# A decoder layer's dense expert stage: one block's sum held in PSUM, value weights in 4 KB packets, gates loaded eight chunks at a time

## The chip, the core and the metric

The kernel runs on one core of one Trainium2 chip. The metric is the time of one execution on the device, in microseconds (us). Engines are named as in the profile: PE is the matrix engine (PEld its weight loads), DVE the vector engine, ACT the scalar engine, POOL the GpSimd engine, SP the sync engine, which here only issues DMAs. The core's DMAs run on 16 DMA engines.

## What is computed

The reference is one post-norm decoder layer over 1024 tokens of width 1024, in float32: a mixer (attention heads beside recurrent heads), then a mixture over 16384 single-neuron experts. The change touches only the latter:

```python
q = (xt @ w_q)...                       # 8 heads, two halves of 128
s = einsum('thpd,hpnd->thpn', q, sub_keys)
...                                     # two top-16 lists, their 256 sums, top 16 of these: idx, gates
def blk(args):                          # a block of 128 tokens, 128 experts per token
    u = u_tab[idx_b]
    h = gelu(einsum('td,ted->te', x_b, u)) * g_b
    return einsum('te,ted->td', h, v_tab[idx_b])
...
x = layer_norm(ALPHA * x + y)
```

## The kernel before

The 1024 tokens are eight blocks of 128. Blocks 0, 1, 6 and 7 (`GATHER`) are done as the reference says: for each of a token's 128 experts POOL issues an indirect DMA that brings one row of 4 KB per partition (a "gather", 512 KB, into a tile named `rows`, of which there are 8). In the u pass DVE multiplies and sums each gathered row with the token (L1124); in the v pass, for blocks 1, 6 and 7, DVE adds each row times its weight to `ys` (L1149).

Blocks 2 to 5 (`DENSE`) are done as dense matrix products over all 16384 experts, 128 experts (a chunk) at a time. The gates have been scattered into a DRAM array `d_g` of shape [16, 128, 128, 32] (32 tokens, expert within the chunk, chunk, token), which is zero where an expert was not chosen. In `dense`, four chunks (`JG`) are a group `g`, 32 groups in all:

- `up(g)`: for each chunk a load of `ur` (512 KB, SP), the split of the weights into a high part `uh` (ACT) and a low part `ul` (DVE, L1032), 24 matmuls into a `psh` bank, the gelu (ACT), the multiplication by the gates `gt` (DVE, L1047) and a split of the product into `hh` and `hl`.
- `down(g)`: for each half of the width (512 columns) and each of the four chunks a load of `vr` (256 KB), its split into `vh` (ACT) and `vl` (DVE, L1032), and 12 matmuls, three for each of the four token blocks, into four PSUM banks (three called `psf`, one `psv`). After the four chunks DVE adds each of the four banks to the sum `y` in SBUF (L1064; the trace calls that tile `dy`).

Three matmuls make one product (`mm3`, L293 to L295: high by high, high by low, low by high). The loop in `dense` interleaves two steps of `down(g-1)`, one step of `up(g)` and a call of `tick`, which emits the gathers' work at a fixed rate per step. So the gathers of blocks 1, 6 and 7 lie beside the dense product all through. A scheduler of the framework then puts each engine's instructions in an order of its own; on the chip each engine runs its list in that order. All loads of the dense product stand in one list, that of SP. Tiles with `bufs=n` rotate through n buffers, and a load waits until the buffer's last reader is done.

When a gathered block is done, `finish` loads its residual into a `rows` tile, adds, and normalizes with the weights `ln_ffn_g` and `ln_ffn_b`. Before the change, these were loaded once early in the dense stage (`dlg`, `dlb`, kept in `self.lnf`) and shared by the three blocks that finish in it and by `finish_dense`, which normalizes blocks 2 to 5 at the very end.

Of the kernel before, what the change touches and what calls it, by code (L numbers as in the profile page):

```python
# [8 lines left out]
F32 = mybir.dt.float32  # L9
# [9 lines left out]
D = 1024  # L19
S = 1024  # L20
P = 128
# [20 lines left out]
QB, PRB = {256: 2, 512: 2}, {2: 3, 4: 7}  # L42
VRAW = 5
PSPL = 1
# [24 lines left out]
GS = float(2 ** 14)  # L69
JG = 4  # L70


class Layer:
    def __init__(self, ctx, tc, a, out, dbg=None):
# [5 lines left out]
        self.hold = 0.0  # L80
        self.lnf = None
        PS = bass.MemoryType.PSUM
# [936 lines left out]
    def dense(self, prep, tail, tl):  # L1019
# [4 lines left out]
        with self.pool("dw", 2, "left") as dw, dws:  # L1024
            dv = {}
            def split(dw, src, n, name, bufs, raws):
                hi = dw.tile([P, n], F32R, name=name + "h", tag=name + "h", bufs=bufs)
                lo = dw.tile([P, n], F32R, name=name + "l", tag=name + "l", bufs=bufs)
                raw = dw.tile([P, n], F32, name=name + "r", tag=name + "r", bufs=raws)
                nc.sync.dma_start(raw, src)  # L1030
                nc.scalar.activation(hi, raw, AF.Copy)  # L1031
                nc.vector.tensor_tensor(lo, raw, hi.bitcast(F32), op=ALU.subtract)  # L1032
                return hi, lo

            def up(g):
                gt = dw.tile([P, TD // 32, JG, 32], F32, name="gt", tag="gt")
                nc.sync.dma_start(gt, self.d_g[:, :, g * JG : (g + 1) * JG, :].rearrange("q j i t -> j q i t"))
                for c in range(JG):
                    hh, hl = (dw.tile([P, TD], F32R, name=n, tag=n, bufs=JG + 2) for n in ("hh", "hl"))
                    uh, ul = (t.rearrange("p (c j) -> p c j", c=DC) for t in split(dw, a["ut"][g * JG + c], D, "u", 2, 3))  # L1040
                    ps = self.bank("h")[:, :TD]
                    for dc in range(DC):
                        self.mm3(ps, uh[:, dc], ul[:, dc], xh[:, dc], xl[:, dc], dc == 0, dc == DC - 1)
                    hs = dw.tile([P, TD], F32, name="hs", tag="hs")
                    nc.scalar.activation(hs, ps, AF.Gelu)  # L1045
                    h3 = hs.rearrange("p (q t) -> p q t", t=32)
                    nc.vector.tensor_tensor(h3, h3, gt[:, :, c], op=ALU.mult)  # L1047
                    nc.scalar.activation(hh, hs, AF.Copy)
                    nc.vector.tensor_tensor(hl, hs, hh.bitcast(F32), op=ALU.subtract)
                    yield hh, hl  # L1050

            def down(g, hs):
# [45 lines left out]
            self.finish_dense(dv[0], y, dv[1])  # L1098

# [101 lines left out]

    def finish_dense(self, pool, y, st):
        nc, V = self.nc, self.nc.vector
        g, b = self.lnf
        mv = pool.tile([P, ND, 2], F32, name="lnmv", tag="lnmv")
# [18 lines left out]
    def finish(self, y, r0):  # L1224
# [25 lines left out]
def layout(inp):  # L1250
# [15 lines left out]
    def ncols(w3, c0, n):  # L1266
# [10 lines left out]
        "wo": c(wo).reshape(4, 2, P, 1024), "wq": c(wq).reshape(16, P, 1024),  # L1277
        "ut": c(np.asarray(inp["peer_u"])[0].reshape(P, P, DC, P).transpose(0, 3, 2, 1)).reshape(P, P, D),
        "kt": c(keys.transpose(2, 0, 1)),
        "u": c(np.asarray(inp["peer_u"])[0]), "v": c(np.asarray(inp["peer_v"])[0]),  # L1280
# [36 lines left out]
```

## Time and profile before

| | us |
|---|---|
| median of 3 runs | 3072.04 |
| lowest and highest | 3071.37, 3078.85 |
| the profiled execution's own time | 3059.49 |
| its span, first to last instruction | 3057.6 |
| PE busy | 2614.2 (85%) |
| DVE busy | 2667.8 (87%) |
| POOL busy | 1612.5 (53%) |
| ACT busy | 1091.4 (36%) |

The profile is one execution, and it is 12.5 us shorter than the median of the runs. Busy time of PE is a sum over pipelined matmuls whose recorded durations overlap the next one, so a PE that is busy all the time may still not be issuing as fast as it can; the number of matmuls in a stretch tells more. The dense stage fills the second half of the span, from about 1500 us.

### The profile page before, as it was taken

How to read it: one execution, taken by the hardware profiler on the slowest of the kernel's cores; microseconds unless marked ns; L12 is line 12 of the kernel's file. 1: busy time of each engine (PE TensorE's matmuls, PEld its weight loads, DVE VectorE, ACT ScalarE, POOL GpSimd, SP SyncE). 2: the span in 40 equal slices, each digit the busy share in tenths (PEclk: the TensorE clock that was granted, in tenths of full speed). 3: DMA queues.
4: the chain of work that ended last, by engine and by line, in shares of the span. 5: the costliest groups of instructions: out<-in, count | busy, mean ns of one | idle time of the engine just before them, and what ended most of it. 6: DMA issues, size and time to landing. Idle time of an engine off the chain costs nothing.

```text
span 3057.6 us, 45196 instructions
## 1 busy us (share of the span) xinstructions
PE 2614.2 (85%) x15865; PEld 2140.4 (70%) x15865; DVE 2667.8 (87%) x5555; ACT 1091.4 (36%) x2068; POOL 1612.5 (53%) x1216
## 2 busy tenths in 40 slices
PE   7778699877669768779578999899989999999995
PEld 6768589755567545568457878777768877877874
DVE  8658776588778998689898999899999999999998
ACT  4733222365312233677522323232223323223321
POOL 2344377655665645110156666565476665656652
PEclk9878899878889879889789999999999999999998
DMA  7632499855877867865589999999999999999994
GB/s 278 195 138 90 178 333 326 256 157 163 303 279 270 288 199 255 312 258 194 192 305 343 361 366 381 333 370 368 345 355 363 372 386 362 359 361 342 371 334 164
DMA packets 338660, 887.11 MB, mean 290 GB/s; under 512 B 29912, under 2 KB 124136, under 8 KB 336000
## 3 DMA queue, kind: packets, MB, share of 16 engines
q0 software_dynamic: 147456, 536.94, 48.3%
q1 hardware_dynamic: 185200, 338.38, 31.7%
q10 hardware_dynamic: 5776, 8.90, 0.8%
q8 instruction: 125, 2.05, 0.3%
q14 instruction: 103, 0.84, 0.1%
HBM read 821.67 MB, written 62.42 MB: 289 GB/s over the span
## 4 chain that ended last, share of the span: by engine, by line
PE 40%; DVE 37%; issue 9%; DMA 6%; ACT 4%; POOL 3%; SPq 0%; DVEq 0%; POOLq 0%; ACTq 0%
DVE ys L1149 7%; PE psf L294 6%; PE psf L295 6%; PE psf L293 5%; DVE rows L1124 5%; PE psh L293 5%; PE psh L295 5%; PE psh L294 5%; POOL rows L1105 2%; DMA rows<-in_u,gsel 1%; DVE tw L808 1%; DVE dy L1064 1%; PE psv L294 1%; PE psv L718 1%; PE psv L295 1%
## 5 line engine op out<-in xcount | busy, mean ns | idle before, releaser
L1105 POOL DMA_INDIRECT rows<-in_u,gsel x512 | 688.4, 1345 | 585.6 <-DVE rows L1124 368.8
L1105 POOL DMA_INDIRECT rows<-in_v,gsel x512 | 640.9, 1252 | 437.7 <-DVE ys L1149 271.2
L1124 DVE SCALAR_TENSOR_TENSOR rows<-rows,gx 128x1024 f32<-128x1024 f32 x512 | 635.6, 1291 | 36.6 <-DMA rows<-in_u,gsel 27.8
L1149 DVE SCALAR_TENSOR_TENSOR ys<-rows,sd,ys 128x1024 f32<-128x1024 f32 x381 | 491.2, 1289 | 0.6
L293 PE MATMUL psh<-dxh,uh 128*128 128x512 f32 x1024 | 403.0, 394 | 29.4 <-ACT uh L1031 16.6
L295 PE MATMUL psh<-dxh,ul 128*128 128x512 f32 x1024 | 401.1, 392 | 9.5 <-DVE ul L1032 9.4
L294 PE MATMUL psh<-dxl,uh 128*128 128x512 f32 x1024 | 400.6, 391 | 0.0
L294 PE MATMUL psf<-vl,hh 128*128 128x512 f32 x768 | 311.0, 405 | 42.2 <-DVE vl L1032 41.4
L1031 ACT ACTIVATE vh<-vr 128x512 fp32r<-128x512 f32 x256 | 161.8, 632 | 436.1 <-PE psv L295 396.1
L295 PE MATMUL psf<-vh,hl 128*128 128x512 f32 x768 | 306.4, 399 | 0.0
L293 PE MATMUL psf<-vh,hh 128*128 128x512 f32 x768 | 278.5, 395 | 10.7 <-DVE dy L1064 8.8
L1031 ACT ACTIVATE uh<-ur 128x1024 fp32r<-128x1024 f32 x128 | 135.8, 1062 | 405.1 <-PE psh L294 400.0
L293 PEld LDWEIGHTS psh<-dxh,uh 128*128 128x128 f32 x1024 | 193.6, 189 | 77.2 <-ACT hs L1045 20.4
L295 PEld LDWEIGHTS psh<-dxh,ul 128*128 128x128 f32 x1024 | 193.5, 189 | 50.4 <-DVE ul L1032 10.5
L294 PEld LDWEIGHTS psh<-dxl,uh 128*128 128x128 f32 x1024 | 193.5, 189 | 39.5
L294 PEld LDWEIGHTS psf<-vl,hh 128*128 128x128 f32 x768 | 148.1, 193 | 89.7 <-DVE vl L1032 59.0
L215 ACT ACTIVATE whi<-wraw 128x1024 fp32r<-128x1024 f32 x106 | 111.6, 1056 | 230.9 <-PE psf L294 64.8
L1032 DVE TENSOR_TENSOR vl<-vr,vh 128x512 fp32r<-128x512 f32 x256 | 170.7, 689 | 12.0 <-ACT vh L1031 11.9
L293 PEld LDWEIGHTS psf<-vh,hh 128*128 128x128 f32 x768 | 145.5, 190 | 48.1 <-DVE dy L1064 9.8
L218 DVE TENSOR_TENSOR wlo<-wraw,whi 128x1024 fp32r<-128x1024 f32 x60 | 81.8, 1365 | 100.8 <-ACT whi L215 98.0
L295 PEld LDWEIGHTS psf<-vh,hl 128*128 128x128 f32 x768 | 148.1, 193 | 29.8
L1032 DVE TENSOR_TENSOR ul<-ur,uh 128x1024 fp32r<-128x1024 f32 x128 | 156.6, 1224 | 11.5 <-ACT uh L1031 10.5
(342 smaller groups left out, 6156.5 us busy)
## 6 DMA issues: line engine op xcount, KB each, us to landing
ur<-in_ut SPq DMA_DIRECT2D x128, 512.0 KB
vr<-in_v SPq DMA_DIRECT2D x256, 256.0 KB
d_g<-slab SPq DMA_DIRECT2D x16, 2048.0 KB
gt<-d_g SPq DMA_DIRECT2D x32, 1024.0 KB
wraw<-in_wq SPq DMA_DIRECT2D x48, 512.0 KB
wraw<-in_wt SPq DMA_DIRECT2D x34, 512.0 KB
wraw<-in_wn SPq DMA_DIRECT2D x24, 512.0 KB
wraw<-in_wo SPq DMA_DIRECT2D x24, 512.0 KB
```

The lines of the kernel that those rows point to most:

```text
L215: nc.scalar.activation(hi, raw, AF.Copy)
L218: eng.tensor_tensor(lo, raw, hi.bitcast(F32), op=ALU.subtract)
L293: mm(out, lh, rh, start=start, stop=False, **kw)
L294: mm(out, lh, rl, start=False, stop=False, **kw)
L295: mm(out, ll, rh, start=False, stop=stop, **kw)
L718: nc.tensor.matmul(pv[:, qb], ps[:, qb * P : (qb + 1) * P], V[:, kb], start=kb == 0, stop=kb == b0 + qb, skip_group_check=True)
L808: nc.vector.match_replace(w, out_v[:, 0:8], vals, FMIN)
L1031: nc.scalar.activation(hi, raw, AF.Copy)
L1032: nc.vector.tensor_tensor(lo, raw, hi.bitcast(F32), op=ALU.subtract)
L1105: self.nc.gpsimd.indirect_dma_start(out=t, out_offset=None, in_=tab, in_offset=bass.IndirectOffsetOnAxis(ap=idx, axis=0))
L1124: self.pin(nc.vector.scalar_tensor_tensor(u, u, 1.0, x2, op0=ALU.mult, op1=ALU.mult, accum_out=sd[:, n : n + 1]), "u")
L1149: self.pin(nc.vector.scalar_tensor_tensor(ys, v, h, ys, op0=ALU.mult, op1=ALU.add), "w")
```

## The change

Five edits, all in the dense stage:

- The sum of the first dense block (`tb == 0`, block 2) is no longer added to `y` after every group. It stays in a two-bank PSUM tile (`whole[0]`, from the pool that block 0's gathered sum used earlier) from the first group to the last, and is added once at the end. The other three blocks use the remaining banks: three `psf` for one half of the width, and `psv`, `psf`, `psf` for the other.
- The dense value weights are read from a second copy of the table, `vt`, prepared on the host, in which two chunks' halves stand side by side: one load of 512 KB with 4 KB per partition takes the place of two of 256 KB with 2 KB. Three buffers (`VRAW`) of that size replace five of the smaller.
- The gates are loaded for eight chunks (`GT`) into one tile, in four parts of 512 KB, one part at every second chunk, ahead of their use. A run of memory is then 1 KB and not 512 B.
- `self.lnf` is gone: each `finish` loads the two normalization rows into `rows` tiles again.
- `finish_dense` gets these rows in two buffers of `ur`, loaded after the last chunk's `ur`.

```diff
-VRAW = 5
+VRAW = 3
+GT = 8
...
+            def gates(m):
+                if m % GT == 1 or m == 0:
+                    gts.append(dw.tile([P, TD // 32, GT, 32], F32, name="gt", tag="gt"))
+                i0 = (len(gts) - 1) * GT
+                for k in range(4) if m == 0 else (m % GT // 2,):
+                    qs = slice(4 * k, 4 * k + 4)
+                    nc.sync.dma_start(gts[-1][:, qs], self.d_g[qs, :, i0 : i0 + GT, :].rearrange("q j i t -> j q i t"))
...
             def up(g):
-                gt = dw.tile([P, TD // 32, JG, 32], F32, name="gt", tag="gt")
-                nc.sync.dma_start(gt, self.d_g[:, :, g * JG : (g + 1) * JG, :].rearrange("q j i t -> j q i t"))
                 for c in range(JG):
+                    m = g * JG + c
+                    if m == 0 or m % 2 and m < P - GT:
+                        gates(m)
...
             def down(g, hs):
+                if g == 0:
+                    whole[0] = self.psy.tile([P, D], F32, name="y", tag="y")
                 for n in range(2):
                     ns = slice(n * 512, (n + 1) * 512)
-                    acc = [self.bank("f") for _ in range(ND - 1)] + [self.bank("v")]
+                    acc = [whole[0][:, ns]] + [self.bank("v" if n and tb == 1 else "f") for tb in range(1, ND)]
                     for c in range(JG):
-                        r0 = (g * JG + c) * P
-                        vh, vl = split(dv[0], a["v"][r0 : r0 + P, ns], 512, "v", 2, VRAW)
+                        if c % 2 == 0:
+                            vr = dv[0].tile([P, 2, 512], F32, name="vr", tag="vr", bufs=VRAW)
+                            nc.sync.dma_start(vr, a["vt"][(g * JG + c) // 2, n].rearrange("p (c d) -> p c d", c=2))
+                        vh, vl = split(dv[0], None, 512, "v", 2, None, vr[:, c % 2])
                         for tb in range(ND):
                             ts = slice(tb * P, (tb + 1) * P)
-                            self.mm3(acc[tb], hs[c][0][:, ts], hs[c][1][:, ts], vh, vl, c == 0, c == JG - 1)
+                            first, last = (g == 0, g == NG - 1) if tb == 0 else (True, True)
+                            self.mm3(acc[tb], hs[c][0][:, ts], hs[c][1][:, ts], vh, vl, first and c == 0,
+                                     last and c == JG - 1, skip_group_check=tb == 0)
                         yield
-                    for tb in range(ND):
+                    for tb in range(0 if g == NG - 1 else 1, ND):
                         nc.vector.tensor_tensor(y[:, tb, ns], y[:, tb, ns], acc[tb], op=ALU.add)
...
-                self.lnf = self.ffn_rows([dv[0].tile([P, D], F32, name=n, tag=n, bufs=1) for n in ("dlg", "dlb")])
...
                 if g == NG - 1:
+                    gb = self.ffn_rows([dw.tile([P, D], F32, name="ur", tag="ur", bufs=3) for _ in range(2)])
...
-        g, b = self.lnf or self.ffn_rows([self.rows() for _ in range(2)])
+        g, b = self.ffn_rows([self.rows() for _ in range(2)])
```

How the order of the instructions moves, at three places. The first is DVE's list in the middle of a v pass (chunks 94 to 95), where it adds gathered rows to `ys` between the dense work. Of the kernel before:

```order
L1047 TENSOR_TENSOR hs<-hs,gt 128x512
L1032 TENSOR_TENSOR vl<-vr,vh 128x512
L1049 TENSOR_TENSOR hl<-hs,hh 128x512
L1149 SCALAR_TENSOR_TENSOR ys<-rows,sd,ys 128x1024
L1064 TENSOR_TENSOR dy<-dy,psf 128x512
L1149 SCALAR_TENSOR_TENSOR ys<-rows,sd,ys 128x1024
L1064 TENSOR_TENSOR dy<-dy,psf 128x512
L1149 SCALAR_TENSOR_TENSOR ys<-rows,sd,ys 128x1024
L1064 TENSOR_TENSOR dy<-dy,psf 128x512
L1149 SCALAR_TENSOR_TENSOR ys<-rows,sd,ys 128x1024
L1064 TENSOR_TENSOR dy<-dy,psv 128x512
```

And of the change, at the same chunks:

```order
L1059 TENSOR_TENSOR hs<-hs,gt 128x512
L1033 TENSOR_TENSOR vl<-vr,vh 128x512
L1084 TENSOR_TENSOR dy<-dy,psv 128x512
L1061 TENSOR_TENSOR hl<-hs,hh 128x512
L1169 SCALAR_TENSOR_TENSOR ys<-rows,sd,ys 128x1024
L1084 TENSOR_TENSOR dy<-dy,psf 128x512
L1169 SCALAR_TENSOR_TENSOR ys<-rows,sd,ys 128x1024
L1084 TENSOR_TENSOR dy<-dy,psf 128x512
L1169 SCALAR_TENSOR_TENSOR ys<-rows,sd,ys 128x1024
L1033 TENSOR_TENSOR vl<-vr,vh 128x512
```

Three adds stand between the gathered rows in place of four, and the next `vl` comes that much sooner; the gathered rows themselves keep their density.

The second place is SP's list in the middle of the stage. Before, one load of gates stood among the loads of weights in every group of four chunks:

```order
L1030 DMA ur<-in_ut 128x1024
L1030 DMA vr<-in_v 128x512 x2
L1037 DMA gt<-d_g 128x16x128
L1030 DMA ur<-in_ut 128x1024
L1030 DMA vr<-in_v 128x512 x2
```

With the change, the four parts that the code spreads over seven chunks stand almost together, once in eight chunks:

```order
L1075 DMA vr<-in_vt 128x1024
L1031 DMA ur<-in_ut 128x1024
L1044 DMA gt<-d_g 128x4x256
L1075 DMA vr<-in_vt 128x1024
L1044 DMA gt<-d_g 128x4x256 x3
L1075 DMA vr<-in_vt 128x1024
L1031 DMA ur<-in_ut 128x1024 x2
L1075 DMA vr<-in_vt 128x1024 x2
```

All four parts fill one tile, so only the first of them waits for the tile's former reader, and the scheduler pulls the rest up behind it: 2 MB in a row where 1 MB stood twice as often.

The third place is SP's list where block 1 is done: `rows<-d_x` (L1227, then L1247) is the residual that `finish` loads, `gsel<-d_sel` the index list of the next block, `out<-rows` the block's result. Before:

```order
L1227 DMA rows<-d_x_211 128x1024
L1113 DMA gsel<-d_sel 128x384
L1030 DMA vr<-in_v 128x512 x2
L1030 DMA ur<-in_ut 128x1024
L1030 DMA vr<-in_v 128x512 x2
L1030 DMA ur<-in_ut 128x1024 x2
L1030 DMA vr<-in_v 128x512
L1037 DMA gt<-d_g 128x16x128
```

And of the change:

```order
L1247 DMA rows<-d_x_211 128x1024
L1133 DMA gsel<-d_sel 128x384
L1254 DMA rows<-in_ln_ffn_g 128x1024
L1254 DMA rows<-in_ln_ffn_b 128x1024
L1075 DMA vr<-in_vt 128x1024
L1031 DMA ur<-in_ut 128x1024
L1075 DMA vr<-in_vt 128x1024
L1031 DMA ur<-in_ut 128x1024
L1250 DMA out<-rows 128x1024
```

Two more loads of `rows` stand ahead of the next weights, and three of the eight `rows` are held until the result goes out, where one was.

## Rows read from the trace of the kernel before

**Rows 1.** The page's first lines: the span, and each engine's busy us, share of the span and instructions.

```profile
span 3057.6 us, 45196 instructions
PE 2614.2 (85%) x15865; PEld 2140.4 (70%) x15865; DVE 2667.8 (87%) x5555; ACT 1091.4 (36%) x2068; POOL 1612.5 (53%) x1216
```

**Rows 2.** Stretches of the dense stage. Columns: from and to, length in us; then busy us and, in brackets, the number of instructions of PE, PEld, DVE, ACT and POOL; granted share of PE's clock; share of time in which packets lay on the 16 DMA engines; GB/s moved. The u passes of blocks 1 and 7 fill 1700:1900 and 2300:2500 but for its end, v passes fill 2000:2200 and 2500:2900.

```profile
1500.00:1600.00 100.00, 70.19 (x285) 55.42 (x286) 85.58 (x159) 25.50 (x36) 44.09 (x30) 0.84 0.79 270
1600.00:1700.00 100.00, 92.19 (x397) 74.98 (x396) 89.57 (x146) 28.65 (x43) 62.88 (x44) 0.97 0.95 339
1700.00:1900.00 200.00, 198.28 (x856) 160.27 (x855) 196.56 (x319) 60.20 (x89) 137.69 (x98) 0.99 1.01 372
1800.00:1900.00 100.00, 99.83 (x438) 81.44 (x437) 98.07 (x160) 30.42 (x45) 67.30 (x48) 1.00 0.99 362
1900.00:2000.00 100.00, 91.23 (x384) 74.00 (x383) 90.47 (x115) 26.40 (x41) 58.53 (x45) 0.95 0.95 348
2000.00:2200.00 200.00, 193.47 (x840) 156.65 (x839) 197.62 (x219) 60.32 (x89) 115.01 (x94) 1.00 0.97 357
2200.00:2300.00 100.00, 89.56 (x375) 71.72 (x375) 96.29 (x160) 27.44 (x40) 64.51 (x48) 0.97 0.98 363
2300.00:2500.00 200.00, 198.05 (x857) 160.69 (x856) 197.15 (x309) 61.31 (x91) 136.36 (x99) 0.99 1.00 371
2500.00:2900.00 400.00, 385.41 (x1664) 312.35 (x1663) 395.90 (x448) 119.08 (x174) 242.56 (x187) 0.99 0.98 360
2900.00:3000.00 100.00, 95.16 (x406) 77.43 (x406) 95.32 (x106) 26.73 (x40) 59.58 (x47) 0.97 0.94 332
3000.00:3040.00 40.00, 24.92 (x94) 18.30 (x92) 35.56 (x61) 5.72 (x9) 7.14 (x5) 0.87 0.33 116
```

**Rows 3.** The chain of work that ended last, by engine and line, as shares of four stretches, in this order: 1700:1900, 2300:2500, 2000:2200, 2500:2900.

```profile
by line: issue 25.6%; DVE rows L1124 13.1%; POOL rows L1105 11.3%; DMA rows<-in_u,gsel 8.9%; PE psh L295 5.1%; PE psh L293 5.1%; PE psh L294 5.0%; PE psf L294 4.5%; PE psf L295 4.2%; PE psf L293 4.2%; DVE dy L1064 3.0%; DVE ul L1032 1.7%; D
...
by line: PE psh L293 12.4%; PE psh L294 12.4%; PE psh L295 12.3%; PE psf L294 11.8%; PE psf L295 11.1%; DVE rows L1124 9.9%; PE psf L293 9.6%; PE psv L294 3.8%; issue 3.7%; PE psv L295 3.4%; PE psv L293 3.2%; DVE ys L1149 2.7%; DVE vl L1032
...
by line: DVE ys L1149 34.3%; issue 14.3%; PE psh L293 5.9%; PE psh L295 5.9%; PE psh L294 5.7%; PE psf L294 5.7%; PE psf L295 5.1%; DVE hs L1047 3.6%; PE psf L293 3.4%; DVE dy L1064 3.4%; DVE vl L1032 2.3%; ACT uh L1031 2.1%; DVE ul L1032 1
...
by line: DVE ys L1149 27.1%; issue 11.9%; PE psh L293 7.7%; PE psh L295 7.6%; PE psh L294 7.5%; PE psf L294 6.7%; PE psf L295 6.2%; PE psf L293 4.5%; DVE dy L1064 2.6%; ACT uh L1031 2.4%; DVE hs L1047 2.3%; PE psv L295 2.0%; PE psv L294 2.0
```

**Rows 4.** Waits between 1600 and 3000 us, of PE and then of DVE: who waited, for whom; us in total, times, longest.

```profile
PE psf L294 <- DVE vl L1032: 39.6, 23, 7.6
PE psh L293 <- ACT hs L1045: 12.3, 16, 2.3
PE psf L293 <- DVE dy L1064: 3.2, 3, 1.6
...
DVE rows L1124 <- DMA gx<-d_x: 7.7, 1, 7.7
...
DVE ys L1147 <- DMA rows<-in_v,gsel: 6.8, 1, 6.8
```

**Rows 5.** The additions to `y` (`dy`), of the whole trace: count, shortest, median and longest in ns, first and last start in us, form.

```profile
L1064 DVE TENSOR_TENSOR dy<-dy,psf x192: 671/680/705, 1584.2 to 3036.7; 128x512 f32<-128x512 f32 x192
L1064 DVE TENSOR_TENSOR dy<-dy,psv x64: 672/682/708, 1586.0 to 3037.3; 128x512 f32<-128x512 f32 x64
```

**Rows 6.** The timeline of DVE in a v pass: start, duration, instruction.

```profile
2506.26 1.28 DVE L1149 SCALAR_TENSOR_TENSOR ys<-rows,sd,ys 128x1024 f32<-128x1024 f32 x1
2507.46 0.68 DVE L1064 TENSOR_TENSOR dy<-dy,psf 128x512 f32<-128x512 f32 x1
2508.06 1.28 DVE L1149 SCALAR_TENSOR_TENSOR ys<-rows,sd,ys 128x1024 f32<-128x1024 f32 x1
```

**Rows 7.** DMA between 1600 and 2900 us: the total; for the gathers' queue (q0) and SP's (q1) packets, MB, and the time of the packets as a share of 16 engines; then loads and gathers, their count, KB each, and for the gathers the median us from issue to landing.

```profile
DMA packets 194702, 469.09 MB, mean 361 GB/s; under 512 B 15646, under 2 KB 73118, under 8 KB 194619
...
q0 software_dynamic: 87303, 317.92, 64.8%
q1 hardware_dynamic: 107316, 150.15, 33.0%
...
vr<-in_v SPq DMA_DIRECT2D x224, 256.0 KB
...
gt<-d_g SPq DMA_DIRECT2D x28, 1024.0 KB
rows<-in_v,gsel POOLq DMA_INDIRECT x334, 8.0
rows<-in_u,gsel POOLq DMA_INDIRECT x274, 8.4
```

**Rows 8.** Instructions on the tile `rows`, of the whole trace (the v pass's sum on DVE; the gathers' times from issue to landing: shortest, median, longest), then between 2205 and 2235 us, where `finish` of block 1 runs.

```profile
L1149 DVE SCALAR_TENSOR_TENSOR ys<-rows,sd,ys x381: 1269/1282/3806, 1929.2 to 3018.4; 128x1024 f32<-128x1024 f32 x191
...
DMA to landing us min/median/max: 4.1/7.7/12.0
...
L1228 DVE SCALAR_TENSOR_TENSOR rows<-rows,ys x1: 1220/1220/1220, 2204.8 to 2204.8; 128x1024 f32<-128x1024 f32 x1
...
L1230 SPq DMA_DIRECT2D out<-rows x1: 344/344/344, 2229.5 to 2229.5; - x1
```

**Rows 9.** The first and the last matmuls of the dense product: of `up`, and of `down` into `psv`.

```profile
L293 PE MATMUL psh<-dxh,uh x1024: 387/390/795, 1504.1 to 2998.7; 128*128 128x512 f32 x171
...
L295 PE MATMUL psv<-vh,hl x256: 388/390/632, 1568.2 to 3035.8; 128*128 128x512 f32 x128
```

More of the change, by code (lines that the diff above doesn't have):

```diff
@@ L80, in __init__ @@
         self.hold = 0.0
-        self.lnf = None
         PS = bass.MemoryType.PSUM
@@ L1025, in dense, with split @@
             dv = {}
-            def split(dw, src, n, name, bufs, raws):
+            def split(dw, src, n, name, bufs, raws, raw=None):
                 hi = dw.tile([P, n], F32R, name=name + "h", tag=name + "h", bufs=bufs)
                 lo = dw.tile([P, n], F32R, name=name + "l", tag=name + "l", bufs=bufs)
-                raw = dw.tile([P, n], F32, name=name + "r", tag=name + "r", bufs=raws)
-                nc.sync.dma_start(raw, src)
+                if raw is None:
+                    raw = dw.tile([P, n], F32, name=name + "r", tag=name + "r", bufs=raws)
+                    nc.sync.dma_start(raw, src)
                 nc.scalar.activation(hi, raw, AF.Copy)
@@ L1033, in split @@
                 return hi, lo
+            gts = []
+            def gates(m):
[5 more added lines that the diff above has]
+                    nc.sync.dma_start(gts[-1][:, qs], self.d_g[qs, :, i0 : i0 + GT, :].rearrange("q j i t -> j q i t"))
             def up(g):
-                gt = dw.tile([P, TD // 32, JG, 32], F32, name="gt", tag="gt")
-                nc.sync.dma_start(gt, self.d_g[:, :, g * JG : (g + 1) * JG, :].rearrange("q j i t -> j q i t"))
                 for c in range(JG):
+                    m = g * JG + c
+                    if m == 0 or m % 2 and m < P - GT:
+                        gates(m)
                     hh, hl = (dw.tile([P, TD], F32R, name=n, tag=n, bufs=JG + 2) for n in ("hh", "hl"))
@@ L1046, in up @@
                     h3 = hs.rearrange("p (q t) -> p q t", t=32)
-                    nc.vector.tensor_tensor(h3, h3, gt[:, :, c], op=ALU.mult)
+                    nc.vector.tensor_tensor(h3, h3, gts[m // GT][:, :, m % GT], op=ALU.mult)
                     nc.scalar.activation(hh, hs, AF.Copy)
@@ L1050, in up @@
                     yield hh, hl
+            whole = [None]
             def down(g, hs):
+                if g == 0:
+                    whole[0] = self.psy.tile([P, D], F32, name="y", tag="y")
                 for n in range(2):
                     ns = slice(n * 512, (n + 1) * 512)
-                    acc = [self.bank("f") for _ in range(ND - 1)] + [self.bank("v")]
+                    acc = [whole[0][:, ns]] + [self.bank("v" if n and tb == 1 else "f") for tb in range(1, ND)]
                     for c in range(JG):
-                        r0 = (g * JG + c) * P
-                        vh, vl = split(dv[0], a["v"][r0 : r0 + P, ns], 512, "v", 2, VRAW)
+                        if c % 2 == 0:
+                            vr = dv[0].tile([P, 2, 512], F32, name="vr", tag="vr", bufs=VRAW)
+                            nc.sync.dma_start(vr, a["vt"][(g * JG + c) // 2, n].rearrange("p (c d) -> p c d", c=2))
+                        vh, vl = split(dv[0], None, 512, "v", 2, None, vr[:, c % 2])
                         for tb in range(ND):
                             ts = slice(tb * P, (tb + 1) * P)
-                            self.mm3(acc[tb], hs[c][0][:, ts], hs[c][1][:, ts], vh, vl, c == 0, c == JG - 1)
+                            first, last = (g == 0, g == NG - 1) if tb == 0 else (True, True)
+                            self.mm3(acc[tb], hs[c][0][:, ts], hs[c][1][:, ts], vh, vl, first and c == 0,
+                                     last and c == JG - 1, skip_group_check=tb == 0)
                         yield
-                    for tb in range(ND):
+                    for tb in range(0 if g == NG - 1 else 1, ND):
                         nc.vector.tensor_tensor(y[:, tb, ns], y[:, tb, ns], acc[tb], op=ALU.add)
@@ L1095, in dense @@
                     dv[1] = dv[0].tile([P, ND, 2, 6], F32, name="lnst", tag="lnst", bufs=1)
+                    gb = self.ffn_rows([dw.tile([P, D], F32, name="ur", tag="ur", bufs=3) for _ in range(2)])
                 if h:
                     prev = down(g, h)
-            self.finish_dense(dv[0], y, dv[1])
+            self.finish_dense(dv[0], y, dv[1], gb)
     def rows(self):
@@ L1200, in gather_v, with finish_dense @@
         self.finish(ys, r0)
-    def finish_dense(self, pool, y, st):
+    def finish_dense(self, pool, y, st, gb):
         nc, V = self.nc, self.nc.vector
-        g, b = self.lnf
+        g, b = gb
         mv = pool.tile([P, ND, 2], F32, name="lnmv", tag="lnmv")
@@ L1278, in layout @@
         "ut": c(np.asarray(inp["peer_u"])[0].reshape(P, P, DC, P).transpose(0, 3, 2, 1)).reshape(P, P, D),
+        "vt": c(np.asarray(inp["peer_v"])[0].reshape(P // 2, 2, P, 2, 512).transpose(0, 3, 2, 1, 4)).reshape(P // 2, 2, P, D),
         "kt": c(keys.transpose(2, 0, 1)),
```

## The prediction

> **What bounds the kernel now.** I read the page's first lines [rows 1], then a table of stretches, then the chain of waits for four of these, then the waits of PE and DVE, and last the DMA queues. The page's shares are means over stages with different limits; only the table by stretches speaks of the dense stage [rows 2].
>
> How fast can PE go? The fullest 100 us hold 438 matmuls [rows 2], so one costs 0.228 us. The dense product has 128 chunks of 24 matmuls up and 24 down, 6144 in all, or 1401 us; it lies between 1504.1 and 3035.8 [rows 9], 1532 us. Where are the 131 us? Count matmuls against 438 per 100 us in each stretch: the first 100 us (the product starts 4 us into them) lack 153 (35 us) and the last 40 lack 81 (18 us), which the change hardly reaches. Between 1600 and 3000 the two u stretches (1700:1900 and 2300:2500) lack 39 of 1752, 8.9 us; the v stretches (2000:2200 and 2500:2900) lack 124 of 2628, 28.3 us; the four stretches of 100 us between them, where a gathered block ends or begins, lack 190 of 1752, 43.3 us. That is 80.5 us, the most that anything could win there.
>
> Who keeps PE from them? In the v stretches DVE is busy 98.8 to 99.0% [rows 2], and the largest piece of the chain is DVE's own adding of gathered rows, 34.3 and 27.1% [rows 3]. In 2300:2500 the chain runs 80% on PE (its nine pieces added), so there PE is the bound. In 1700:1900 it goes round the gathers, POOL issue, DMA, DVE. PE's own waits say the same: 39.6 us for `vl`, which stands in DVE's list behind gathered rows, 12.3 us for the gelu, and only 3.2 us for `dy` to clear a bank [rows 4]. The DMA engines are covered 0.97 to 1.01 of the time [rows 2]. Three resources lie within some per cent of each other, so a relief of one is cut short by the next.
>
> **The adds.** Each of 31 groups loses two of eight additions; the last keeps all. 256 (192 and 64) [rows 5] become 194, 62 fewer. One lasts 0.68 us, but the next instruction starts 0.60 us after it does [rows 6]. So DVE gets 62 x 0.60 = 37.2 us back, or 42.3 by the full duration, evenly from 1584 to 3000, 2.6 us in every 100. The v stretches are 600 us: 15.8 us, and I take all, since DVE ends the waits there and PE lacks 28.3. What is late next is PE: it would lack 2.1 us in 100, as in the u stretches now (8.9 in 400). The u stretches are 400 us: 10.5 us of relief, of which I take a third, 3.5, because PE or the gathers' round trip is the bound. The 400 us between: 10.5 us, and I take half, 5.2, since DVE itself waits there for DMAs (7.7 and 6.8 us [rows 4]) and time freed before such a wait only lengthens it. Together **24.5 us**. Below, 8 (half of the v stretches alone); above, 42.3.
>
> On PE nothing is added: the same 6144 matmuls. A sum over 32 groups in one bank has no row; the nearest are the `psh` matmuls, 24 of them in one sum, with a median of 390 ns, like those of `psv` [rows 9], sums of 12. I take no difference. The wait for `dy` mostly goes, and is inside the 24.5.
>
> **The value loads.** The bytes stay; 256 loads become 128. The lead stays as well: five half-chunk buffers leave four filled while one loads, three double ones also four, half of a group of eight half-chunks. A group takes about 46 us (192 x 0.228 = 43.8, longer by the 80.5 in 1400 that PE lacks), so 23 us against gathers that land in 8.0 [rows 7]. I take nothing. If that cover were gone, ACT's `vh`, then DVE's `vl`, would be late.
>
> Longer packets: the gathers' queue, of 4 KB packets but for small index reads, needs 64.8% of 16 x 1300 us for 317.92 MB, 42.4 engine-us per MB; SP's queue 45.7 [rows 7]. If all of SP's 150.15 MB cost the lower price, each engine would save 31 us in 1300. But `vr` and `gt` are only 59 and 29 MB of it, and the gates reach 1 KB. I estimate 10 us. That is room, not path: in no stretch's chain but 1700:1900 does a DMA show a share, 8.9% [rows 3], and that is a gather. So 0 in the sum; the bounds are 0 and, if DMA ends the waits after the relief, 10.
>
> The Trainium skill ("DMA: Bandwidth & Descriptors", Specifications) puts line rate at transfers of 512 B and more. By that neither the 512 B nor the 2 KB packets leave anything to gain; the row's 42.4 against 45.7 says that something is left. By the rule this term is exactly 0, by the row up to 31 us of engine time.
>
> **The gates.** SP's list has the four parts nearly together, 2 MB every eight chunks for 1 MB every four. At 372 GB/s, the most in a stretch [rows 2], the burst lasts 5.6 us for 2.8. Behind the first part's wait for the tile's last reader stand the other parts and the next weights, which keep the 23 us above. More exposed are the gathers: one starts every 2.04 us (98 in 200) to 2.14 (187 in 400) [rows 2], so a `rows` buffer comes round in 16.3 to 17.1 us and needs 8.0 to 8.4 to land [rows 7] and 1.28 on DVE [rows 8]: some 7 us are spare. The longest landing of any gather is 12.0 [rows 8]; 2.8 more and 1.28 make 16.1, just inside. I take 0; above, 15 bursts x 2.8 = 42 us.
>
> **The normalization rows.** `finish` of block 1 runs from 2204.8 to 2229.5 [rows 8]. Three of eight `rows` are held, not one. Five come round in 10.2 us; landing and use take 8.4 + 1.28 = 9.7. That fits; at the longest landing they are 3.1 us late a round, 2.4 rounds, 7.5 us, and two blocks (1 and 6) end inside the stage: 0 to 15. I take 2, near the medians. On SP the two loads stand behind the residual and the index list, whose waits come first anyway. Block 7's last row is added at 3018.4 [rows 8], and the dense sum ends at 3037 [rows 5], so its rows, and those in `ur` for `finish_dense`, are covered by the last group: 0.
>
> **The start.** 2 MB of gates instead of 1 stand ahead of the first `ur`: 0 to 2.8 us. I take 1.
>
> **Sum.** 24.5 - 2 - 1 = 21.5 us. The profiled execution took 3059.5, so it would take 3038. The median of the runs lies 12.5 higher; I carry that over: 3072.0 - 21.5 = **3050**.
>
> **Rivals.** *All of the relief counts.* Any 62 adds less on a DVE that is 98% busy shorten it by their full 42.3 us, and shorter packets give DMA room. For it: DVE is at 98 to 99% in all full stretches. Against it: the 80% on PE in 2300:2500. It gives 3072 - 42 = 3030.
>
> *DMA is the ceiling.* The engines are covered 0.97 to 1.01 of the time. 15.8 us less in 600 us would raise the v stretches from 357 and 360 to some 369 GB/s, just under the 372 of 1700:1900. If what they move now is all they can, only the 10 us of packets count, and less the costs of 3 it is 3065, or with the estimate halved 3069: no difference that can be told (0.3%, 9.2 us, is about what a measurement of this kernel can tell). The Trainium skill (the same page, "Where 436 GB/s comes from") has the HBM side bind at about 358 GB/s per core. By that the v stretches are at the limit and the time stays at 3072; the 372 of a 200 us stretch disagrees.
>
> *The bursts of gates starve the gathers.* DVE waits in order for a gathered row, `vl` stands behind it, PE behind `vl`. 15 bursts cancel the gain and 9.2 us more when each holds DVE up by 2.0 us; at 4 us the time is 3050 + 60 = 3110. For it: the 16.1 of 16.3 us above. Against it: a typical landing leaves 7 us.
>
> **How the numbers follow.** Chances: forecast 0.50, full relief 0.20, DMA ceiling 0.19, bursts 0.11. The first two are faster by over 0.3% (below 3062.8), the third the same, the last slower. The range goes from 3024 (full relief, and 6 us more from the stretches between) to 3074 (ceiling, with costs); outside lie the bursts and a little of the full relief.
>
> **What the next profile would show.** 194 additions to `dy`. In the v stretches 422 to 430 matmuls per 100 us (418 now), DVE busy below 98%, and a larger share of PE in the chain; in 2300:2500's like no change to speak of. SP's queue nearer to 42.4 engine-us per MB. The wait for `dy` near nothing and that for `vl` well under 39.6. Gathers landing as now, at 8, with some at 10 to 14 after the gates. I would be wrong if DVE began to wait for gathered rows by more than some 10 us in all (bursts, or the held rows), if a stretch moved no more than 360 GB/s with packets on the engines all the time (ceiling), or if PE lacked hardly anything in every stretch (full relief).

## The result, and the profile after

The changed kernel takes 3056.23 us (median of 6 runs, 3048.52 to 3060.54) where the kernel before takes 3079.07 beside it (6 runs, 3071.37 to 3082.60). The ratio is 0.9925, with a 95% interval of 0.9908 to 0.9941: 23 us less, where 21.5 were forecast. A second comparison, on the chip of three of the experiments, gave 0.9914 (0.9890 to 0.9939). So the size was right; the time itself is 6 us above the forecast 3050, because the kernel before took 3079.07 here and not 3072.04. The terms that add up to the size were not right, as the stretches and the experiments show.

The two profiled executions differ by 4.3 us only (spans 3057.6 [rows 1] and 3053.3):

```profile
span 3053.3 us, 44668 instructions
...
PE 2611.2 (86%) x15865; PEld 2145.2 (70%) x15865; DVE 2630.9 (86%) x5493; ACT 1091.9 (36%) x2068; POOL 1632.1 (53%) x1216
```

They must be compared from the first matmul of the dense product on. It starts at 1504.1 before [rows 9] and here, after code that the change does not touch, at 1518.9. In the other profiles below that start lies anywhere from 1484.7 to 1515.4, so the lateness is a variation of the first half, and each profile is read relative to its own start. From there to the last `psf` matmul it is 1531 us before and 1513 after.

The tiles `dy` (the additions) and `y` (the new PSUM sum), of the whole trace after; columns as in [rows 5]:

```profile
L1084 DVE TENSOR_TENSOR dy<-dy,psf x160: 671/678/689, 1596.9 to 3032.9; 128x512 f32<-128x512 f32 x160
L1084 DVE TENSOR_TENSOR dy<-dy,psv x32: 672/680/689, 1619.1 to 3030.5; 128x512 f32<-128x512 f32 x32
...
L1084 DVE TENSOR_TENSOR dy<-dy,y x2: 683/686/689, 3005.6 to 3029.8; 128x512 f32<-128x512 f32 x2
...
L293 PE MATMUL y<-vh,hh x256: 387/389/632, 1577.0 to 3029.0; 128*128 128x512 f32 x128
```

The additions are 194, as counted. A matmul in the sum that runs over all 32 groups lasts 389 ns in the median, like those in `psf`, which are in sums of 12. This trace does not show when the gathers land. That of the second profile of the same kernel (after_again, below) does, as in [rows 8]:

```profile
DMA to landing us min/median/max: 4.1/7.6/13.2
```

The median is that of before (7.7); the longest is 13.2 for 12.0. In e1_sum and e2_vt, which load the gates as before, it is 14.2 and 13.3, so the longer tail is not a sign of the gates.

Waits between 1600 and 3000 us after, columns as in [rows 4], and SP's and the gathers' queue between 1600 and 2900, as in [rows 7]:

```profile
PE y L294 <- DVE vl L1033: 37.9, 12, 16.3
...
PE psf L293 <- DVE dy L1084: 9.0, 4, 5.9
...
DVE ys L1167 <- DMA rows<-in_v,gsel: 7.4, 2, 6.4
...
DVE rows L1144 <- DMA rows<-in_u,gsel: 6.3, 8, 1.6
```

```profile
DMA packets 151995, 475.54 MB, mean 366 GB/s; under 512 B 14488, under 2 KB 43288, under 8 KB 151917
...
q0 software_dynamic: 88217, 321.24, 65.5%
q1 hardware_dynamic: 63700, 153.32, 31.8%
```

PE's wait for `vl` has the same total as before (37.9 for 39.6), but it comes 12 times and not 23, and the longest is 16.3 for 7.6. In the three v stretches below it falls from 11.7 to 4.3 us; most of it now stands where gathered blocks change: 16.3 at the end of block 1, 6.4 where block 7 goes from u to v, 5.3 at the end of block 6. The stretches are cut at nearly the same points of the program (the same matmul of the dense product's 6144, to within 24), and not at the same times. Before (columns as in [rows 2]; three stretches in v passes, two with u passes, then the switch of block 1 from u to v, its end, the switch of block 7 from u to v, and the end of block 6):

```profile
1942.00:2170.00 228.00, 222.85 (x967) 181.77 (x966) 223.75 (x248) 68.51 (x101) 134.66 (x107) 0.99 0.99 365
2498.00:2726.00 228.00, 221.03 (x960) 179.12 (x959) 225.19 (x249) 68.43 (x101) 132.39 (x108) 1.00 0.99 362
2784.00:2968.00 184.00, 178.39 (x771) 145.74 (x771) 178.88 (x198) 54.33 (x80) 122.33 (x87) 0.98 0.97 357
1653.00:1890.00 237.00, 227.55 (x976) 183.77 (x975) 224.06 (x364) 67.85 (x100) 158.41 (x111) 0.98 0.98 358
2273.00:2454.00 181.00, 180.56 (x788) 146.73 (x788) 177.85 (x287) 54.66 (x81) 122.76 (x87) 1.00 1.00 370
1890.00:1942.00 52.00, 43.23 (x180) 34.46 (x179) 45.16 (x69) 13.86 (x21) 32.18 (x23) 0.93 0.90 330
2170.00:2273.00 103.00, 91.18 (x380) 72.38 (x379) 99.07 (x152) 27.70 (x40) 61.60 (x47) 0.97 0.94 343
2454.00:2498.00 44.00, 42.49 (x181) 34.36 (x180) 43.78 (x61) 13.42 (x21) 27.60 (x22) 0.97 1.03 394
2726.00:2784.00 58.00, 52.36 (x215) 41.41 (x214) 57.79 (x75) 16.00 (x23) 31.14 (x26) 0.94 0.96 345
```

After, the same nine:

```profile
1943.00:2169.00 226.00, 224.80 (x986) 185.40 (x986) 222.18 (x243) 69.06 (x102) 148.11 (x111) 0.99 0.99 375
2505.00:2724.00 219.00, 217.62 (x958) 179.06 (x957) 218.11 (x238) 67.54 (x100) 154.78 (x108) 1.00 0.99 371
2787.00:2964.00 177.00, 174.81 (x768) 143.48 (x767) 173.92 (x189) 54.40 (x80) 108.19 (x85) 1.00 0.96 358
1671.00:1898.00 227.00, 222.86 (x962) 180.35 (x961) 218.93 (x352) 68.21 (x100) 153.26 (x110) 0.98 0.98 365
2274.00:2452.00 178.00, 177.26 (x774) 144.12 (x774) 173.55 (x281) 54.74 (x81) 124.88 (x87) 1.00 1.00 380
1898.00:1943.00 45.00, 40.66 (x171) 32.23 (x170) 42.26 (x65) 12.59 (x19) 32.48 (x23) 0.95 0.99 371
2169.00:2274.00 105.00, 88.53 (x379) 71.81 (x378) 94.76 (x146) 28.15 (x41) 60.86 (x45) 0.92 0.91 333
2452.00:2505.00 53.00, 46.61 (x192) 37.82 (x192) 44.78 (x60) 13.74 (x21) 31.89 (x25) 0.90 0.96 355
2724.00:2787.00 63.00, 51.55 (x200) 40.88 (x199) 53.12 (x70) 15.05 (x22) 33.84 (x26) 0.86 0.92 333
```

Take from each length its matmuls at 0.228 us, and what is left is the time that PE lost:

| stretch | before | after | difference |
|---|---|---|---|
| three v stretches | 7.5 + 9.1 + 8.2 | 1.2 + 0.6 + 1.9 | -21.1 |
| u stretches | 14.5 + 1.3 | 7.7 + 1.5 | -6.6 |
| block 1, u to v | 11.0 | 6.0 | -5.0 |
| end of block 1 | 16.4 | 18.6 | +2.2 |
| block 7, u to v | 2.7 | 9.2 | +6.5 |
| end of block 6 | 9.0 | 17.4 | +8.4 |

In the v passes PE now runs at 434 to 437 matmuls per 100 us, where the fullest 100 us before had 438 [rows 2]; the gain there is nearly everything that was to be had. It is also more than the additions themselves: these stretches are 14 groups, so 28 additions or 16.8 us at 0.60 have gone from them, and PE gains 21.1. DVE's own idle time there (length less busy) falls too, from 12.2 to 7.8 us.

But at the last three changes of block 17 us come back. Most of what PE loses there is waiting, and some is a lower clock after it. PE at the end of block 6, after a wait of 4.3 us, and then the stretch in which it is busy all the time with 38 matmuls in 10 us, at a granted clock of 0.82:

```profile
2742.53 0.80 PE L294 MATMUL y<-vl,hh 128*128 128x512 f32 x1 [4.32 <-DVE vl L1033]
...
2743.97 0.63 PE L295 MATMUL psv<-vh,hl 128*128 128x512 f32 x1
2744.40 0.63 PE L294 MATMUL psf<-vl,hh 128*128 128x512 f32 x1
...
2752.51 0.39 PE L294 MATMUL y<-vl,hh 128*128 128x512 f32 x1
2752.74 0.39 PE L295 MATMUL y<-vh,hl 128*128 128x512 f32 x1
```

```profile
2744.00:2754.00 10.00, 10.00 (x38) 8.13 (x37) 7.92 (x16) 2.15 (x3) 5.10 (x4) 0.82 0.87 295
```

At the lower of the clock's two levels (1.2 and not 2.4 GHz) matmuls start some 0.43 us apart here, not 0.23. In the whole of this end (2724 to 2787) 28 starts lie 0.3 to 0.7 us behind the one before; what they take beyond 0.228 adds up to 5.9 of the 17.4 us.

What begins the wait at the switch of block 7 is seen on DVE (timeline: start, duration, instruction, and in brackets the idle time before it and what ended it):

```profile
2462.59 0.72 DVE L1033 TENSOR_TENSOR vl<-vr,vh 128x512 fp32r<-128x512 f32 x1
2469.69 0.75 DVE L1167 TENSOR_SCALAR ys<-rows,sd 128x1024 f32<-128x1024 f32 x1 [6.38 <-DMA rows<-in_v,gsel]
```

The first value row of the block stands in DVE's list right behind a `vl`, and DVE waits 6.4 us for its gather with the next `vl` behind it. After it come the block's last five u rows. In the kernel before, that value row stood behind them, and DVE did not wait for it. In e1_sum, which has the sum alone, DVE waits 6.3 us at the same row: the order came with the sum.

### The profile page after: what moved, and what is told of

It reads as the page before. It is cut to its first block, busy times and chain, and to the rows that moved or that the text cites. A ratio compares the mean times of both kernels' runs of the same rounds, so it can differ in the third digit from the quotient of the medians.

```text
span 3053.3 us, 44668 instructions
## 1 busy us (share of the span) xinstructions
PE 2611.2 (86%) x15865; PEld 2145.2 (70%) x15865; DVE 2630.9 (86%) x5493; ACT 1091.9 (36%) x2068; POOL 1632.1 (53%) x1216
## 4 chain that ended last, share of the span: by engine, by line
PE 43%; DVE 29%; issue 11%; DMA 7%; POOL 6%; ACT 4%; SPq 0%; another core or an unknown queue 0%; DVEq 0%; POOLq 0%; ACTq 0%
PE psf L294 6%; PE psf L295 6%; PE psf L293 5%; POOL rows L1125 5%; PE psh L295 5%; PE psh L293 5%; PE psh L294 5%; DVE rows L1144 4%; DVE ys L1169 3%; DMA rows<-in_v,gsel 2%; DMA rows<-in_u,gsel 1%; PE psv L718 1%; DVE tw L808 1%; PE y L294 1%; PE y L295 1%
## 5 line engine op out<-in xcount | busy, mean ns | idle before, releaser
L1125 POOL DMA_INDIRECT rows<-in_v,gsel x512 | 668.8, 1306 | 407.7 <-DVE ys L1169 208.1
L294 PE MATMUL psf<-vl,hh 128*128 128x512 f32 x640 | 253.7, 396 | 0.0
L295 PE MATMUL psf<-vh,hl 128*128 128x512 f32 x640 | 253.5, 396 | 0.0
L293 PE MATMUL psf<-vh,hh 128*128 128x512 f32 x640 | 239.4, 396 | 14.4 <-DVE dy L1084 14.3
L293 PEld LDWEIGHTS psf<-vh,hh 128*128 128x128 f32 x640 | 121.3, 189 | 46.2 <-DVE dy L1084 21.2
L218 POOL TENSOR_TENSOR wlo<-wraw,whi 128x1024 fp32r<-128x1024 f32 x46 | 112.4, 2447 | 70.8 <-ACT whi L215 68.1
L294 PE MATMUL y<-vl,hh 128*128 128x512 f32 x256 | 106.4, 416 | 43.1 <-DVE vl L1033 43.1
```

Of the source, the lines that this page charges most:

```text
L218: eng.tensor_tensor(lo, raw, hi.bitcast(F32), op=ALU.subtract)
L293: mm(out, lh, rh, start=start, stop=False, **kw)
L294: mm(out, lh, rl, start=False, stop=False, **kw)
L295: mm(out, ll, rh, start=False, stop=stop, **kw)
L1125: self.nc.gpsimd.indirect_dma_start(out=t, out_offset=None, in_=tab, in_offset=bass.IndirectOffsetOnAxis(ap=idx, axis=0))
```

## The experiments

All ratios are to the kernel before on the same chip, each run in five rounds. "Stage" is the time from the dense product's first matmul into `psh` to its last into `psf` in that kernel's profile (1531 us for the kernel before). It is one execution: that of e1_sum, for one, is the fastest of its six (3029.0), and kernels whose ratios can't be told apart (e1_sum, e7_sum_vt) differ by 10 us in it.

| kernel | edits | median us | ratio | 95% interval | stage us |
|---|---|---|---|---|---|
| e1_sum | sum | 3036.53 | 0.9942 | 0.9921 to 0.9963 | 1509 |
| e2_vt | weights | 3056.98 | 1.0007 | 0.9993 to 1.0021 | 1534 |
| e3_gates | gates, rows | 3064.40 | 1.0027 | 1.0012 to 1.0043 | 1538 |
| e4_rows | rows | 3067.98 | 1.0039 | 1.0024 to 1.0054 | 1544 |
| e5_nogates | sum, weights, rows | 3033.63 | 0.9932 | 0.9909 to 0.9955 | 1518 |
| e6_nosum | weights, gates, rows | 3062.90 | 1.0030 | 1.0016 to 1.0044 | 1542 |
| e7_sum_vt | sum, weights | 3037.27 | 0.9940 | 0.9918 to 0.9962 | 1519 |
| after_again | all | 3029.40 | 0.9914 | 0.9890 to 0.9939 | 1512 |
| e8_dummy | all, and 62 dummy additions | 3077.10 | 1.0019 | 1.0009 to 1.0030 | 1539 |
| e9_half | all, half the sum | 3062.08 | 0.9973 | 0.9960 to 0.9987 | 1524 |
| e10_own | rows loaded anew, own tiles | 3068.36 | 0.9992 | 0.9980 to 1.0003 | 1533 |
| e11_fx | all, residual in its own tile | 3043.20 | 0.9908 | 0.9891 to 0.9924 | 1506 |

The kernel before had medians of 3056.45 beside the first four, 3054.49 beside the next four and 3071.02 beside the last four. "Sum", "weights", "gates" and "rows" are the edits of the diff above, taken whole; the "rows" edit has `finish` load the normalization rows into gather buffers, and `finish_dense` into `ur`.

**One edit at a time.** The theory was the forecast: the sum gives the gain, the rest costs 3 us. The rivals were that DMA is the ceiling (then packets count) and that the gates' bursts starve the gathers.

> The kernel before with one of the five edits: the first dense block's sum stays in PSUM (62 additions fewer); weights, gates and normalization rows are loaded as before. If DVE's relief carries the gain, this alone takes 20 to 25 us off (ratio 0.992 to 0.9935), and each steady group of the dense stage is PE's alone, about 44 us. If the whole gain needs the longer packets too (DMA ends the waits once DVE is relieved), it takes off 10 to 15 (0.995 to 0.997). If all relief counts, 37 to 42 (0.986 to 0.988).

> The kernel before with the value weights alone in 4 KB packets. By the forecast nothing (0.997 to 1.003), with SP's queue costing fewer engine-us per MB. If the DMA engines are the ceiling, 5 to 10 us off (0.997 or less).

> The kernel before with the gates of eight chunks in four parts and, since the tiles would not fit otherwise, the normalization rows loaded by each finish. By the forecast 3 us more (1.001), against e4_rows 1 us. If the bursts of 2 MB starve the gathers, 2 to 4 us for each of 15 bursts, 30 to 60 us more than e4_rows (1.01 to 1.02).

> The kernel before with the normalization rows alone loaded by each finish into gather buffers. By the forecast 2 us more (1.0007, not to be told from 1). By the upper bound, or if the held buffers are what gives time back where blocks 1 and 6 end, 8 to 15 us more (1.0025 to 1.005), seen as longer groups there.

The sum alone gives 18 to 20 us (ratio, medians). The packets of the weights alone give nothing that can be told. The gates beside the rows are not slower than the rows alone (3064.4 against 3068.0, intervals that overlap, and DVE's list is the same in both), so there is no sign of starving. The surprise is e4_rows: 11.5 us where 2 were forecast. By these the whole change would come to 0.9976; it came to 0.9914 and 0.9925, so the edits don't add up.

**What the edits do within the change.**

> The changed kernel with the gates loaded as before (1 MB for every four chunks). If the gates' edit does nothing, as the difference of e3_gates and e4_rows says (0.9988), the time is the changed kernel's, 0.9925 to 0.996 of before. If the shorter packets (512 B) matter only once DVE is relieved, it is 5 to 10 us slower than the changed kernel.

> The changed kernel with the 62 additions put back. If the edits add up, it is e3_gates with the value weights' packets, 1.002 to 1.004 of before, and the sum is worth 0.9942 within the change as well as alone. If the sum is worth more beside the longer packets, the difference to the changed kernel exceeds 20 us.

> The kernel before with the sum in PSUM and the value weights in 4 KB packets, the normalization rows kept for all finishes and gates as before. If the packets do nothing (e2_vt), it is e1_sum again, 0.994. If DMA ends the waits once DVE is relieved, 5 to 10 us better than e1_sum, 0.991 to 0.9925.

> The changed kernel again, on the chip of the three others. By the first comparison 0.9925 of before. If the single edits add up (0.9942 for the sum, 1.0007 for the packets, 1.0027 for gates and rows together), 0.9976.

Put back into the changed kernel, the additions cost 33.5 us (3062.90 less 3029.40), against 20 that they give alone. The rows cost nothing beside the sum (e5_nogates against e7_sum_vt, 0.9932 and 0.9940). The packets add nothing to the sum either (e7_sum_vt is e1_sum again). With the gates as before the changed kernel takes 4.2 us more, again within the intervals.

DVE's lists in the traces say why the edits don't add up. Laid side by side, from the kernel before to e4_rows some 57 of the 2183 DVE instructions of the dense stage move to another place, and e6_nosum keeps that list. From e1_sum to the changed kernel only 5 of 2121 move. So the order that the rows bring (its cost is read below) stands in e4_rows and e6_nosum, and not beside the sum. The sum itself, however, moves some 830 others besides the 62 that it removes: no run has the old order without the additions, so none gives their time apart from the order written without them.

**Is it DVE's time?** Fewer additions also leave PSUM banks without a wait to be cleared. The next two keep the banks and give DVE the time back, and do half of the sum.

```diff
+                    if g < NG - 1:
+                        nc.vector.tensor_tensor(dv[2], y[:, 0, ns], y[:, 1, ns], op=ALU.add)
                     for tb in range(0 if g == NG - 1 else 1, ND):
```

> The changed kernel with 62 additions of the same size put back on DVE, which read and write SBUF only (two of y's blocks into a spare tile), one where each removed addition stood; the sum stays in PSUM. If the gain is DVE's time and nothing else, it is e6_nosum again: 1.000 to 1.003 of before. If the banks that no longer wait to be cleared carry part of it, it stays at 0.993 to 0.998.

```diff
+                    keep = n == 0
...
-                            first, last = (g == 0, g == NG - 1) if tb == 0 else (True, True)
+                            first, last = (g == 0, g == NG - 1) if tb == 0 and keep else (True, True)
...
-                    for tb in range(0 if g == NG - 1 else 1, ND):
+                    for tb in range(0 if g == NG - 1 or not keep else 1, ND):
```

> The changed kernel with the first dense block's sum held in PSUM for one half of the width only: 31 additions fewer than before in place of 62. If the gain is proportional, half of the way from e6_nosum (1.003) to the changed kernel (0.9914 to 0.9925): 0.997 to 0.998. If PE is the bound soon after the first relief, most of the gain is there already: 0.992 to 0.995.

62 additions to a tile that nobody reads bring the time of e6_nosum back (1.0019 against 1.0030), with the sum in PSUM all the while. So the gain is not the banks', and DVE's time is enough for it. The control isn't pure: some 620 of DVE's other instructions stand elsewhere than in the changed kernel, and what that order costs or gives is not split off. Half of the additions give about half of the way (0.9973; the middle of 1.0030 and 0.992 is 0.9975). One addition is worth 33.5 / 62 = 0.54 us against e6_nosum, 0.47 to 0.52 by the ratios (1.0019 of e8_dummy, 0.9925 and 0.9914 of the changed kernel), and only 0.29 to 0.32 in the kernel before (e1_sum). So it has no fixed price.

**What do the rows cost?**

```diff
-                self.lnf = self.ffn_rows([dv[0].tile([P, D], F32, name=n, tag=n, bufs=1) for n in ("dlg", "dlb")])
+                self.lnf = dv[0]
...
-        g, b = self.lnf
+        g, b = self.own_rows()
...
+    def own_rows(self):
+        return self.ffn_rows([self.lnf.tile([P, D], F32, name=n, tag=n, bufs=1) for n in ("dlg", "dlb")])
```

> The kernel before, with the normalization rows loaded anew for each finish, but into two tiles of their own and not into gather buffers; DVE's list is that of before word for word. If the 12 us of e4_rows come from the held buffers or from the order that the scheduler then wrote, 0.999 to 1.001. If they come from the loads themselves, ahead of the weights on SP's queue, 1.003 to 1.004.

```diff
-        x2 = self.rows()
+        x2 = self.fx.tile([P, D], F32, name="fx", tag="fx", bufs=1) if self.fx else self.rows()
```

> The changed kernel with the residual of finish in a tile of its own, so that two of eight gather buffers are held and not three. If held buffers cost what the forecast took (2 us for two), it is the changed kernel, within 0.001. If they cost the 12 us of e4_rows, 4 to 6 us faster than the changed kernel, with shorter groups where blocks 1 and 6 end.

The loads cost nothing that can be told (e10_own, 0.9992). Where e4_rows loses its time is seen in two groups of block 7's v pass, the dense product's matmuls 4033 to 4416 in every kernel: the kernel before, e4_rows, e6_nosum, e10_own, and then e1_sum, one row each (the counts take in matmuls that touch an edge).

```profile
2511.48:2603.39 91.91, 88.58 (x386) 71.72 (x385) 90.63 (x102) 27.39 (x41) 51.56 (x42) 1.00 0.99 365
```

```profile
2503.59:2603.16 99.57, 91.78 (x385) 73.88 (x384) 90.74 (x101) 27.21 (x41) 55.62 (x43) 0.97 0.93 342
```

```profile
2502.94:2603.46 100.52, 92.75 (x385) 74.69 (x385) 90.74 (x101) 27.23 (x40) 54.75 (x43) 0.95 0.91 333
```

```profile
2524.17:2615.99 91.82, 88.50 (x386) 71.69 (x385) 90.59 (x102) 27.39 (x41) 51.54 (x42) 1.00 0.99 364
```

```profile
2496.08:2583.31 87.23, 87.23 (x386) 71.92 (x385) 86.97 (x96) 27.02 (x41) 59.29 (x44) 1.00 1.01 383
```

384 matmuls at 0.228 are 87.6 us. PE loses 4.4 us before, 12.0 in e4_rows and 13.0 in e6_nosum, 4.3 in e10_own, and none in e1_sum. No `finish` runs in these groups, so no held buffer delays them. What differs is DVE's list, which the scheduler wrote anew: in e10_own it is that of before (two `vl` early in the stage apart). In e4_rows as many gathered rows (151) stand ahead of one of the `ul`, but the last of them are added sooner and none stands right before it. DVE reaches it 3.3 us too early for ACT, with the rows that could be added queued behind it:

```profile
2518.35 0.28 DVE L1134 TENSOR_TENSOR sd<-sd,gsel 128x128 f32<-128x128 f32 x1
2521.94 1.23 DVE L1031 TENSOR_TENSOR ul<-ur,uh 128x1024 fp32r<-128x1024 f32 x1 [3.31 <-ACT uh L1030]
```

The kernel before, at the same `ul`, waits 0.16:

```profile
2524.14 1.28 DVE L1149 SCALAR_TENSOR_TENSOR ys<-rows,sd,ys 128x1024 f32<-128x1024 f32 x1
2525.59 1.23 DVE L1032 TENSOR_TENSOR ul<-ur,uh 128x1024 fp32r<-128x1024 f32 x1 [0.16 <-ACT uh L1031]
```

DVE's waits for ACT's `uh` in the two groups, of e4_rows and then of the kernel before (columns as in [rows 4]):

```profile
DVE ul L1031 <- ACT uh L1030: 6.8, 2, 3.5
```

```profile
DVE ul L1032 <- ACT uh L1031: 0.2, 1, 0.2
```

In all DVE stands idle 8.8 us there in e4_rows and 1.3 before (length less busy), which is nearly all of the 7.7 us by which the groups are longer. So 7.7 us of what e4_rows loses (12 us in the stage, 11.5 in the medians) is an order that a DVE at 98% cannot catch up with. Most of the rest lies in the two groups where blocks 1 and 6 end, 4.5 and 1.0 us longer. In the first DVE waits for gathered rows, in e4_rows and then before:

```profile
DVE rows L1123 <- DMA rows<-in_u,gsel: 7.0, 3, 3.6
```

```profile
DVE rows L1124 <- DMA rows<-in_u,gsel: 0.8, 1, 0.8
```

That is what held buffers would do, but the list differs too, and no run parts the two. e11_fx does not settle it: the group in which block 6 ends (matmuls 4993 to 5184) takes 58.4 us in after_again (three of eight held), 55.4 in e11_fx (two), but 59.9 in e7_sum_vt and 55.1 in e1_sum (one each), so its time does not follow the number held. In the time as a whole e11_fx (0.9908) can't be told from the changed kernel (0.9914, 0.9925); it is the fastest against its own kernel before.

## Why the prediction came out right

The mechanism was right: DVE ended the waits in the v passes, taking its additions away gave the time, and neither DMA nor the bursts took their place. That the sum comes within 2 us is in part luck, since its terms have no fixed size. Counted from the kernel before, the additions alone give 18 to 20 us where 24.5 were forecast, and the other edits, forecast to cost 3, take 5 to 9 off beside them (0.9942 against 0.9925 and 0.9914, intervals that overlap). Counted in the other order, the rows cost 11.5 us where 2 were forecast, and the additions beside them are worth 33.5. Either way two errors cancel.

- **Relief, 24.5 us from 62 x 0.60.** The whole lies between what the two orders give, 18 to 20 and 33.5; the "full relief" of 42.3, which had 0.20, was not reached. The shares were mis-sized. The v stretches (640 us here, 600 in the forecast) gave 21.1 and not 15.8: PE there fell to losing 0.6 to 1.9 us in about 200, where the 2.1 in 100 of the u stretches had been taken as what is left. The u stretches gave 6.6 and not 3.5. The 400 us between were taken as a gain of 5.2. There the four changes of block in the table lost 12 on balance; at the switch of block 7 it is as the argument had it ("time freed before such a wait only lengthens it").
- **The rows, 2 us.** This step failed for the kernel before: 11.5 there. The prediction had looked only at the buffers and the queue of SP. It missed that the edit lets the scheduler rewrite DVE's list some hundred us away, where 7.7 us go into waits of an engine that has no slack. Beside the sum that order does not arise: e1_sum takes 87.2 us for those two groups and the changed kernel 87.7 (at 379 GB/s), what 384 matmuls need.
- **Value loads, 0.** Right (1.0007). The queue's room was larger than estimated: SP's queue fell from 45.7 to 31.8% x 16 x 1300 / 153.32 = 43.1 engine-us per MB, against 42.4 of the gathers'. On 150 MB that is some 24 us for each engine, where 10 were estimated (with the gates'), and still it gave no time.
- **Gates, 0, and the start, 1.** No cost was seen. Both comparisons (e3_gates with e4_rows, e5_nogates with after_again) put the gates some 4 us on the gaining side, within their intervals. The rival of the bursts falls: e3_gates isn't slower than e4_rows, and the gathers of the changed kernel land at 7.6 in the median (after_again; 7.7 before).
- **DMA as the ceiling.** This falls too. Two v stretches went from 365 and 362 GB/s to 375 and 371 (the third from 357 to 358), and a u stretch to 380 over 178 us. The 358 GB/s that the Trainium skill gives as the HBM side's limit for a core ("DMA: Bandwidth & Descriptors", "Where 436 GB/s comes from") does not bind here, with one core at work.
- **Signs.** Four were wrong. The v stretches were to reach 422 to 430 matmuls per 100 us; they reached 434 to 437. DVE was to fall below 98% in them; it stayed at 98 to 99.6 of each, since the groups became shorter with its work: both engines are now full. The wait for `vl` was to fall well under 39.6 us; it moved to the changes of block and is 37.9. And the wait for `dy` was to go; it rose from 3.2 to 9.0 us, 5.9 of them at the end of block 6. One could not be read: DVE waits 13.7 us for gathered rows (7.4 and 6.3), over the some 10 that were to speak for the bursts or the held rows, but it was 10.0 before (6.8 and 3.2).

The lost time at the switch of block 7 is named (DVE's wait for the first value row, in the changed kernel's list). Whether another order would save it was not tried.

## What to carry to other kernels

When two engines are both within a per cent or two of full, taking work from the one that ends the waits paid here, but at no fixed price: 62 additions of 0.60 us to issue gave 0.3 us each in one list and 0.54 in another. Compare stretches cut at the same points of the program, since what is won in the steady part partly comes back where the work changes kind. An edit that costs nothing in loads or bytes can still make the scheduler write another list, and on an engine without slack that costs more than the edit: hold the list against the old one before trusting a zero.

## What was not expected of the hardware

Behind an addition of 0.68 us on DVE the next instruction starts 0.60 us after it does [rows 6]. Two sums into `ys` with an addition between them are 1.80 us apart [rows 6]; three that stand in a row take 3.92 us in the changed kernel, or some 1.3 each and not 1.20:

```profile
2544.62 3.92 DVE L1169 SCALAR_TENSOR_TENSOR ys<-rows,sd,ys 128x1024 f32<-128x1024 f32 x3
```

Each reads what the one ahead of it wrote; that this is the reason was not tested. It costs little here: such neighbours stand 17 times in the dense stage before and 19 times after.

The half of the program ahead of the dense stage, the same in all kernels, reached the first dense matmul between 1484.7 and 1518.9 us in 14 profiles, more than the whole change is worth. Much of that goes by chip: 1493.5 to 1496.0 in e1_sum to e4_rows, 1512.6 to 1515.4 in e8_dummy to e11_fx, each four kernels on one chip, but 1484.7 to 1497.5 in the four between. So ratios are taken on one chip, and profiles from the dense product's first matmul.
